# Hybrid decoder layer: the state-space stage rearranged between engines, and the low halves of the weights on VectorE

## The chip, the core and the metric

The kernel runs on one core of one Trainium2 chip. That core has TensorE (PE in the profile, with PEld for its weight loads), VectorE (DVE), ScalarE (ACT), GpSimd (POOL), SyncE (SP, which here only issues DMAs) and DMA queues. Each engine works through its own instructions in order and waits on semaphores for the others. The metric is the time of one execution in device microseconds. The kernel before takes 1495.65 us, the median of three runs from 1494.98 to 1497.01 us.

## The reference

The layer takes x of 512 tokens by 1024 channels, float32:

```
h = rms_norm(x); u = h @ w_in                  # 1024 x 11512
y_a = dsa(u)     # 16 heads, each query sees 128 keys picked by an index
y_b = nsa(u)     # 16 heads: compressed, selected and window branches
y_c = ssd(u)     # state space: 32 heads of 64, 4 groups, chunks of 128 tokens
x = x + (sig(g_a) * y_a@Wa + sig(g_b) * y_b@Wb + sig(g_c) * y_c@Wc) @ w_out
x = x + relu(rms_norm(x) @ w_1)^2 @ w_2
```

The part around the change is the state-space branch:

```
xbc  = silu(causal_conv(xbc, w, width 4) + b)      # per channel
a_cum = cumsum(dt * a) within a chunk
lmat = exp(where(i >= j, a_cum[i] - a_cum[j], -inf))
y    = (C B^T * lmat * dt) @ x  +  exp(a_cum) * (C @ h_in)  +  x * d_skip
y    = rms_norm(y * silu(z))
```

## The kernel before

All large products are computed in three passes: both operands are split into a high part (type fp32r, a rounded float32) and a low part, the remainder, and `mm3` (L316 to L319) issues high x high, high x low (or low x high) and the other mixed product into one PSUM tile `pj` of 128x512. Weights are streamed. SP issues the DMA of a tile of up to 128x1024 (`wraw`, 3 buffers), `split` (L139 to L153) makes `whi` on ACT (L150) and `wlo = wraw - whi` on POOL (L151), 6 buffers each, three tiles ahead of the use. There are 212 such tiles.

Two streams of instructions are merged into one program. The **filler** is all large products in a fixed list (`FORD`, then merge gates, branches, w_out, feed-forward): a chunk of it is eight tiles of 128 rows times three passes, 24 matmuls into one of two `pj` buffers. The **main stream** is the index of the first attention (DVE-heavy, L722 to L733), that attention (16 units), the state-space stage (16 units of one group and one chunk of tokens), and the second attention (32 units). Program order comes from a debt: each yield of the main stream gives a number of ns, which the filler works off. A scheduler then orders each engine's instructions by a priority (the main stream's is raised by `HM`) and by its own model of times. At run time those orders are fixed, and only semaphores move the engines against each other.

The filler's convolution `conv` (L676 to L700) works on one `pj` of 128 channels by 512 tokens. ACT copies it to `craw` (L679) and makes the first tap (L681), after which `pj` is free; DVE adds three taps from `craw` (L684, in SBUF), ACT makes a tanh (L686), DVE the product (L688), and for most channels PE transposes the result.

A state-space unit has three stages. `stage1` loads: `E`, 128x8x128, is a broadcast of the cumulated sums; `xs`, `zs`, and B and C. `stage2`: PE multiplies C and B into a `pT` tile, DVE multiplies it by `tri25` (0.25 where allowed, else 0) into `cbm` (L1100); DVE subtracts the head's own sum from each of the 8 parts of `E` and takes the minimum with 0 (L1102); ACT takes the exponential of all of `E` (L1103); POOL scales `xs` to `xt`, `xw` and `xd` (L1105, L1108, L1112); DVE multiplies `E` by `cbm` (L1110). `stage3`: products with the state (L1121, L1127) and eight products `xt` x `E` (L1137), then DVE adds `xd` (L1141), the state's part `t1` (L1143) and multiplies by `zs` (L1144).

An attention unit goes back and forth: PE scores (L755, L756), DVE mask and maximum (L757), ACT exponential (L764), DVE reciprocal and scaling (L770 to L777, every fourth head on POOL, L775), PE transposes (L791), ACT and DVE the two halves (L795, L796), PE the product with the values (L803, L804). `pipeline` overlaps the scores of a unit with the rest of the one before it. After the last unit the branch `b1` stores `yt`, reads it back as `yr` (L664) and splits it (L665, L666). Branch `b1` and all that follows it can't be computed earlier.

Of the kernel before, what the change touches and what calls it, by code (L numbers as in the profile page):

```python
# [14 lines left out]
S = 512  # L15
# [21 lines left out]
def build_kernel(ctx, tc, A, out):  # L37
# [44 lines left out]
    # ------------------------------------------------------------------ constants  # L82
# [37 lines left out]
    # ------------------------------------------------------------------ weights  # L120
    class WS:
# [19 lines left out]
        def split(s):  # L141
# [9 lines left out]
            pool.tensor_tensor(lo[:, :m], r[:, :m], f(hi[:, :m]), op=ALU.subtract)  # L151
# [76 lines left out]
    # first weights run ahead of the activations  # L228
# [4 lines left out]
    # ------------------------------------------------------------------ small constants  # L233
# [31 lines left out]
    # ------------------------------------------------------------------ x -> h^T  # L265
# [19 lines left out]
    tri25 = tri("tri25", 128, 0.0, 0.25, 0, -1, 1)  # L285
# [29 lines left out]
    # ------------------------------------------------------------------ matmul helpers  # L315
# [50 lines left out]
    # ------------------------------------------------------------------ persistent attention operands  # L366
# [86 lines left out]
    # ------------------------------------------------------------------ filler: all large products  # L453
# [30 lines left out]
    def cmp_prep(u1, e1):  # L484
        """k_cmp and v_cmp operands from the raw kc, vc columns."""
# [189 lines left out]
    # ------------------------------------------------------------------ conv + silu of the SSD inputs  # L675
    def conv(m, p):  # L676
        cw = lambda k: convc[:, k * 24 + m:k * 24 + m + 1]
        raw = stg.tile([128, S], F32, name="craw", tag="r", bufs=RB)
        act.activation(raw, p, AF.Copy)  # L679
        acc = stg.tile([128, S], F32, name="cacc", tag="acc", bufs=AB)  # L680
        act.activation(acc, p, AF.Identity, scale=cw(3), bias=convc[:, 96 + m:97 + m])  # L681
        for k in range(3):
            sh = 3 - k
            dve.scalar_tensor_tensor(acc[:, sh:], raw[:, :S - sh], cw(k), acc[:, sh:], op0=ALU.mult, op1=ALU.add)  # L684
        th = stg.tile([128, S], F32, name="cth", tag="th", bufs=TB)
        act.activation(th, acc, AF.Tanh, scale=0.5)  # L686
        so = raw
# [17 lines left out]
    # ------------------------------------------------------------------ DSA index and its top 128  # L705
# [33 lines left out]
    # ------------------------------------------------------------------ attention units  # L739
# [126 lines left out]
    # ------------------------------------------------------------------ NSA  # L866
# [4 lines left out]
    def cmp_a(b, g, q2, ratio):  # L871
        """Compressed-branch softmax of 8 heads and the block choice."""
# [142 lines left out]
    # ------------------------------------------------------------------ SSD  # L1015
    def ssd_prelude():
# [27 lines left out]
        for k in ("dth", "acm", "dw", "ea", "dec"):  # L1044
            sv[k] = cp.tile(n, F32, name="sv_" + k)
# [9 lines left out]
        dve.tensor_copy(sv["acm"], p[:, 0:128])  # L1055
        act.activation(sv["dec"], p[:, 128:256], AF.Exp)
# [14 lines left out]
    def ssd(sv, ratio):  # L1071
# [22 lines left out]
        def stage2(u):  # L1094
# [5 lines left out]
            dve.tensor_tensor(cbm, p[:, :128], tri25, op=ALU.mult)  # L1100
            for h in range(8):
                dve.tensor_scalar(u.E[:, h], u.E[:, h], col(sv["acm"], c, g)[:, h:h + 1], 0.0, op0=ALU.subtract, op1=ALU.min)  # L1102
            act.activation(u.E, u.E, AF.Exp)  # L1103
# [11 lines left out]
        def stage3(u):  # L1115
# [3 lines left out]
            if c:  # L1119
                po = ps("sc", [128, 512])  # L1120
                pe.matmul(po, u.b[:, 2], hst[g], start=True, stop=True)  # L1121
                t1 = sp.tile([128, 512], F32, name="t1", bufs=2)
                dve.tensor_tensor(x3(t1), x3(po), bc(col(sv["ea"], c, g)[:, :, None], [128, 8, 64]), op=ALU.mult)
                yield ratio * 858
# [16 lines left out]
            dve.tensor_tensor(yv, py, u.xd, op=ALU.add)  # L1141
            if c:
                dve.tensor_tensor(yv, yv, t1, op=ALU.add)  # L1143
# [55 lines left out]
    # ------------------------------------------------------------------ branches, merge, w_out, feed-forward  # L1199
    def branches(ya):  # L1200
# [94 lines left out]
        # w_out + residual + norm2  # L1295
# [169 lines left out]
```

## Time and profile before

| | |
|---|---|
| timed runs | 1494.98, 1495.65, 1497.01 us |
| the profiled execution: span from its first to its last instruction | 1496.3 us |
| its own time | nothing stands beside the span; it lies between the second and the third timed run |
| busy PE, PEld | 1400.1 us (94%), 1149.9 us (77%) |
| busy DVE, ACT, POOL | 1013.8 us (68%), 691.0 us (46%), 715.6 us (48%) |
| mean granted clock of TensorE | 0.978 |
| HBM traffic | 194.6 MB, 130 GB/s |

Busy is the union of an engine's instructions. PE's matmuls are pipelined and their ends are modelled, so a busy PE is not at its peak: in the feed-forward part, where nothing interrupts it, it starts a 512-wide matmul every 0.226 us (442 in 100 us). [...] A wait is idle time of an engine before an instruction, put down to what came last.

### The profile page before, as it was taken

Reading aid. Unit: us, or ns where it says so; the run is one execution under the profiler, and the core shown is the slowest. Engines: PE = TensorE matmul, PEld = TensorE weight load, DVE = VectorE, ACT = ScalarE, POOL = GpSimd, SP = SyncE. Lnnn points to the kernel's source line nnn. Section 1 sums busy time; section 2 is a strip of 40 time slices with the busy share of each in tenths; the row PEclk is TensorE's granted clock in tenths of the full one; section 3 lists DMA queues with packets and bytes.
Section 4 is the critical chain, followed back from the end, with each engine's and each line's share of the span. In section 5 each row is a group of like instructions: output and inputs, shape, how many; then the busy total and the mean of one; then the engine's idle time right before and its main releaser. Section 6 shows DMA issues by size and latency. Waiting matters only on the chain.

```text
span 1496.3 us, 19760 instructions
## 1 busy us (share of the span) xinstructions
PE 1400.1 (94%) x6832; PEld 1149.9 (77%) x6832; DVE 1013.8 (68%) x1887; ACT 691.0 (46%) x1364; POOL 715.6 (48%) x456
## 2 busy tenths in 40 slices
PE   6998999899988898899999999999999999999999
PEld 5886788677866676787788877777678888888887
DVE  4699956789789987757767898786645751433411
ACT  4545445667644454545555555545333441422220
POOL 5544534434245366544334765644753542544351
PEclk9999999999999998999999999999999999999999
DMA  5323464443565565654324744422652322323231
GB/s 194 99 77 106 150 203 130 125 122 94 139 198 173 166 199 159 200 170 130 106 89 147 206 140 117 117 78 78 211 201 82 113 99 71 127 73 112 83 106 50
DMA packets 218272, 195.92 MB, mean 131 GB/s; under 512 B 15664, under 2 KB 165564, under 8 KB 218172
## 3 DMA queue, kind: packets, MB, share of 16 engines
q1 hardware_dynamic: 212700, 183.12, 41.3%
q0 software_dynamic: 4608, 8.39, 2.0%
q10 hardware_dynamic: 864, 3.15, 0.5%
q8 instruction: 54, 0.88, 0.2%
q14 instruction: 46, 0.38, 0.1%
HBM read 157.85 MB, written 36.77 MB: 130 GB/s over the span
## 4 chain that ended last, share of the span: by engine, by line
PE 56%; DVE 29%; ACT 5%; DMA 5%; issue 4%; POOL 2%; SPq 0%; DVEq 0%; ACTq 0%; POOLq 0%
PE pj L318 15%; PE pj L319 15%; PE pj L317 15%; DVE E L1102 3%; DVE cacc L684 3%; DVE p L777 3%; ACT p L764 3%; DVE ptl L796 2%; DVE mask L731 2%; DVE m L730 1%; DVE p L757 1%; PE pT L791 1%; PE sc L1137 1%; PE sc L755 1%; DMA wraw<-in_w_in_dram 1%
## 5 line engine op out<-in xcount | busy, mean ns | idle before, releaser
L151 POOL TENSOR_TENSOR wlo<-wraw,whi 128x1024 fp32r<-128x1024 f32 (+3 forms) x212 | 479.0, 2269 | 416.7 <-ACT whi L150 394.9
L150 ACT ACTIVATE whi<-wraw 128x1024 fp32r<-128x1024 f32 (+3 forms) x212 | 207.3, 982 | 210.9 <-PE pj L319 102.1
L319 PE MATMUL pj<-hTh,wlo 128*128 128x512 f32 x384 | 156.8, 408 | 0.0
L317 PE MATMUL pj<-hTh,whi 128*128 128x512 f32 x384 | 155.4, 405 | 0.1
L318 PE MATMUL pj<-hTl,whi 128*128 128x512 f32 x384 | 154.8, 403 | 0.0
L764 ACT ACTIVATE p<-p,nb,rs 128x256 f32<-128x256 f32 (+3 forms) x192 | 123.3, 644 | 59.2 <-DVE nb L762 58.9
L317 PE MATMUL pj<-whi,hTh 128*128 128x512 f32 (+2 forms) x352 | 138.7, 396 | 8.1 <-DVE zo L575 2.2
L318 PE MATMUL pj<-wlo,hTh 128*128 128x512 f32 (+2 forms) x352 | 138.7, 395 | 0.8 <-POOL wlo L151 0.8
L319 PE MATMUL pj<-whi,hTl 128*128 128x512 f32 (+2 forms) x352 | 139.0, 396 | 0.0
L1363 DVE TENSOR_TENSOR fr<-fr 128x512 f32<-128x512 f32 x32 | 80.8, 2530 | 56.2 <-ACT fr L1362 56.2
L1371 DVE TENSOR_TENSOR x<-x,pj 128x512 f32<-128x512 f32 x32 | 22.0, 687 | 138.3 <-PE pj L319 137.8
L777 DVE TENSOR_SCALAR p<-p,rc 128x256 f32<-128x256 f32 (+3 forms) x144 | 113.3, 837 | 1.1
L775 POOL TENSOR_TENSOR p<-p,rc 128x256 f32<-128x256 f32 (+3 forms) x48 | 37.9, 790 | 152.5 <-DVE rc L770 51.8
L317 PE MATMUL pj<-yh,whi 128*128 128x512 f32 x256 | 103.4, 406 | 5.1 <-DVE gld L1282 3.1
L318 PE MATMUL pj<-yl,whi 128*128 128x512 f32 x256 | 103.6, 405 | 0.2 <-DVE yl L666 0.2
L319 PE MATMUL pj<-yh,wlo 128*128 128x512 f32 x256 | 103.0, 402 | 0.0
L318 PE MATMUL pj<-wlo,fh 128*128 128x512 f32 x256 | 99.6, 389 | 0.0
L319 PE MATMUL pj<-whi,fo 128*128 128x512 f32 x256 | 99.6, 389 | 0.0
L317 PE MATMUL pj<-whi,fh 128*128 128x512 f32 x256 | 98.8, 389 | 0.0
L319 PE MATMUL pj<-h2h,wlo 128*128 128x512 f32 (+1 forms) x256 | 96.2, 376 | 0.0
L318 PE MATMUL pj<-h2l,whi 128*128 128x512 f32 (+1 forms) x256 | 96.2, 376 | 0.0
L317 PE MATMUL pj<-h2h,whi 128*128 128x512 f32 (+1 forms) x256 | 96.1, 376 | 0.0
(333 smaller groups left out, 3322.5 us busy)
## 6 DMA issues: line engine op xcount, KB each, us to landing
wraw<-in_w_in_dram SPq DMA_DIRECT2D x84, 512.0 KB, 4.1
wraw<-in_w_ff_dram SPq DMA_DIRECT2D x64, 512.0 KB, 4.0
gld<-g_d SPq DMA_DIRECT2D x48, 256.0 KB, 3.1
q_d<-qev SPq DMA_DIRECT2D x32, 256.0 KB, 2.3
qu<-q_d POOLq DMA_DIRECT2D x32, 256.0 KB, 4.2
E<-ac_d SPq DMA_DIRECT2D x16, 512.0 KB, 4.3
wraw<-in_w_br_ssd_dram SPq DMA_DIRECT2D x16, 512.0 KB, 4.2
g_d<-gth SPq DMA_DIRECT2D x24, 256.0 KB, 2.0
```

Of the source, the lines that this page charges most:

```text
L150: act.activation(hi[:, :m], r[:, :m], AF.Copy)
L151: pool.tensor_tensor(lo[:, :m], r[:, :m], f(hi[:, :m]), op=ALU.subtract)
L317: pe.matmul(o, lh, rh, start=first, stop=False)
L318: pe.matmul(o, lh, rl, start=False, stop=False)
L319: pe.matmul(o, ll, rh, start=False, stop=last)
L684: dve.scalar_tensor_tensor(acc[:, sh:], raw[:, :S - sh], cw(k), acc[:, sh:], op0=ALU.mult, op1=ALU.add)
L731: dve.match_replace(wk, m8, wk, TAKEN)
L764: act.activation(u.p[h][:, :n], u.p[h][:, :n], AF.Exp, bias=u.nb[:, h:h + 1], scale=rs8[:, u.b, u.h0 + h:u.h0 + h + 1], accum_out=u.sm[:, ...
L775: pool.tensor_tensor(u.p[h][:, :n], u.p[h][:, :n], bc(rc[:, h:h + 1], [128, n]), op=ALU.mult)
L777: dve.tensor_scalar(u.p[h][:, :n], u.p[h][:, :n], rc[:, h:h + 1], None, op0=ALU.mult)
L1102: dve.tensor_scalar(u.E[:, h], u.E[:, h], col(sv["acm"], c, g)[:, h:h + 1], 0.0, op0=ALU.subtract, op1=ALU.min)
L1363: dve.tensor_tensor(r, r, r, op=ALU.mult)
```

## The change

Five edits. In `conv` the copy L679 goes, and the three taps read `pj` in PSUM. In the state-space unit `cbm` is made on ACT with a plain factor of 0.25; the triangle is applied to `E` by a select on POOL (fill -1e30); the head's own sum comes in as the bias of eight exponentials of 128x128 on ACT, from a new table `nac` of negated sums, in place of eight DVE instructions and one wide exponential. The skip term is added to `t1` on POOL, so that DVE adds once to the product. And `wlo` of every weight tile is computed on DVE. Line numbers after L285 are lower by one to three in the changed file.

```diff
-            pool.tensor_tensor(lo[:, :m], r[:, :m], f(hi[:, :m]), op=ALU.subtract)
+            dve.tensor_tensor(lo[:, :m], r[:, :m], f(hi[:, :m]), op=ALU.subtract)
...
-    tri25 = tri("tri25", 128, 0.0, 0.25, 0, -1, 1)
...
-        raw = stg.tile([128, S], F32, name="craw", tag="r", bufs=RB)
-        act.activation(raw, p, AF.Copy)
         acc = stg.tile([128, S], F32, name="cacc", tag="acc", bufs=AB)
...
-            dve.scalar_tensor_tensor(acc[:, sh:], raw[:, :S - sh], cw(k), acc[:, sh:], op0=ALU.mult, op1=ALU.add)
+            dve.scalar_tensor_tensor(acc[:, sh:], p[:, :S - sh], cw(k), acc[:, sh:], op0=ALU.mult, op1=ALU.add)
...
-        so = raw
+        so = stg.tile([128, S], F32, name="craw", tag="r", bufs=RB)
...
+        dve.tensor_scalar(sv["nac"], p[:, 0:128], -1.0, None, op0=ALU.mult)
...
-            dve.tensor_tensor(cbm, p[:, :128], tri25, op=ALU.mult)
+            act.activation(cbm, p[:, :128], AF.Copy, scale=0.25)
+            pool.affine_select(out=u.E, in_=u.E, compare_op=ALU.is_ge, fill=NEG, base=0,
+                               pattern=[[0, 8], [1, 128]], channel_multiplier=-1)
             for h in range(8):
-                dve.tensor_scalar(u.E[:, h], u.E[:, h], col(sv["acm"], c, g)[:, h:h + 1], 0.0, op0=ALU.subtract, op1=ALU.min)
-            act.activation(u.E, u.E, AF.Exp)
+                act.activation(u.E[:, h], u.E[:, h], AF.Exp, bias=col(sv["nac"], c, g)[:, h:h + 1])
...
                 dve.tensor_tensor(x3(t1), x3(po), bc(col(sv["ea"], c, g)[:, :, None], [128, 8, 64]), op=ALU.mult)
+                pool.tensor_tensor(t1, t1, u.xd, op=ALU.add)
...
-            dve.tensor_tensor(yv, py, u.xd, op=ALU.add)
-            if c:
-                dve.tensor_tensor(yv, yv, t1, op=ALU.add)
+            dve.tensor_tensor(yv, py, t1 if c else u.xd, op=ALU.add)
             dve.tensor_tensor(yv, yv, u.zs, op=ALU.mult)
```

The scheduler orders all engines anew. Numbers in the names below tell buffers apart. On DVE, in the state-space stage, one unit's work stood like this before:

```order
L1141 TENSOR_TENSOR yv_4432<-sc_4390,xs_4184 128x512
L1143 TENSOR_TENSOR yv_4432<-yv_4432,t1_4393 128x512
L1144 TENSOR_TENSOR yv_4432<-yv_4432,zs_4186 128x512
L1100 TENSOR_TENSOR cbm_4362<-pT_4360,tri25_269 128x128
L1110 TENSOR_TENSOR E_4275<-E_4275,cbm_4362 128x1024
L1102 TENSOR_SCALAR E_4350<-E_4350,sv_acm_663 128x128 x8
```

and in the changed program, where `t1` already holds the skip term:

```order
L1122 TENSOR_TENSOR t1_5305<-sc_5303,sv_ea_662 128x512
L1109 TENSOR_TENSOR E_5110<-E_5110,cbm_5199 128x1024
L473 TENSOR_TENSOR qev_5867<-pF_5856,qev_5867 64x2x128
L151 TENSOR_TENSOR wlo_6358<-wraw_6170,whi_6357 128x1024
L1141 TENSOR_TENSOR yv_5333<-sc_5302,t1_5305 128x512
L1142 TENSOR_TENSOR yv_5333<-yv_5333,zs_5114 128x512
```

The eight instructions on `E`, `cbm` and the second addition have left DVE, and a `wlo` stands in it. The second place is DVE in the first attention, where the convolutions run between attention work. Before, the three taps of a chunk (L684) read `craw`:

```order
L684 SCALAR_TENSOR_TENSOR cacc_3946<-craw_3944,convc_297,cacc_3946 128x509
L688 SCALAR_TENSOR_TENSOR craw_3895<-cth_3902,cacc_3897 128x512
L684 SCALAR_TENSOR_TENSOR cacc_3946<-craw_3944,convc_297,cacc_3946 128x510
L796 TENSOR_TENSOR ptl_3246<-pT_3240,pth_3245 128x512
L811 TENSOR_TENSOR yt_3201<-pv_3161,yt_3201 64x512
L684 SCALAR_TENSOR_TENSOR cacc_3946<-craw_3944,convc_297,cacc_3946 128x511
```

Now (as L681) they read `pj`:

```order
L681 SCALAR_TENSOR_TENSOR cacc_3933<-pj_3894,convc_294,cacc_3933 128x509
L754 ISA p_3019,mx_3015<-sc_3018,mask1_696 128x256
L754 ISA mx_3015 128x1
L759 SCALAR_TENSOR_TENSOR nb_2929<-mx_2928,rs8_322 128x4
L681 SCALAR_TENSOR_TENSOR cacc_3933<-pj_3894,convc_294,cacc_3933 128x510
L767 RECIPROCAL rc_2920<-smx_2810 128x4
L685 SCALAR_TENSOR_TENSOR craw_3892<-cth_3890,cacc_3885 128x512
L681 SCALAR_TENSOR_TENSOR cacc_3933<-pj_3894,convc_294,cacc_3933 128x511
```

The `pj` buffer is now released by the last of the three, with attention work of other units between them, where ACT alone released it before. The third place is PE at the end of the second attention. Before, the scores of the last unit (`qu_9996`) and the products with the values stand among the filler's matmuls into `pj`, which go on behind them:

```order
L755 MATMUL sc_10467<-kh_s1_307,qu_9996 128x128
L756 MATMUL sc_10467<-kl_s1_308,qu_9996 128x128
L803 MATMUL pv_10397<-pth_10447,v_s1_314 128x512
L804 MATMUL pv_10397<-ptl_10448,v_s1_314 128x512
L318 MATMUL pj_9765<-yl_9759,whi_9593 128x512
L319 MATMUL pj_9765<-yh_9758,wlo_9594 128x512
L318 MATMUL pj_9792<-yl_9759,whi_9662 128x512
L319 MATMUL pj_9792<-yh_9758,wlo_9663 128x512
```

In the changed program the last unit ends like this, and the next `pj` is the first of branch `b1`:

```order
L788 MATMUL pT_10531<-ident_105,p_10475 128x128 x2
L940 MATMUL pv_10508<-cph_10267,vz_321 128x128 x4
L800 MATMUL pv_10508<-pth_10518,v_w1_313 128x512
L801 MATMUL pv_10508<-ptl_10519,v_w1_313 128x512
L800 MATMUL pv_10508<-pth_10536,v_s1_311 128x512
L801 MATMUL pv_10508<-ptl_10537,v_s1_311 128x512
L316 MATMUL pj_10567<-yh_10483,whi_10015 128x512
L316 MATMUL pj_10568<-yh_10483,whi_10067 128x512
```

Between the last `pj` of branch `b0` and that first one of `b1`, PE has 120 attention matmuls in a row; before, no more than 22 stand together anywhere. Counted in matmuls into `pj` that stand ahead, the first attention starts at 751 (before: 662), the state-space products at 1416 (1306), the second attention at 1928 (1776), and its last product with the values stands at 2880 (2856), where `b0` ends at 2880 in both.

## Rows read from the trace of the kernel before

**Rows 1.** Windows: length, busy us of PE, PEld, DVE, ACT, POOL, clock, DMA, GB/s.

```profile
60.00:200.00 140.00, 126.91 (x651) 104.68 (x650) 129.10 (x291) 63.84 (x140) 67.58 (x38) 0.98 0.40 121
...
200.00:420.00 220.00, 208.73 (x1040) 171.79 (x1038) 164.51 (x340) 138.04 (x279) 89.56 (x58) 0.99 0.50 134
...
420.00:640.00 220.00, 188.41 (x911) 148.53 (x912) 190.17 (x300) 107.16 (x218) 121.19 (x79) 0.91 0.62 181
...
860.00:1060.00 200.00, 186.46 (x912) 150.91 (x911) 167.20 (x351) 101.30 (x228) 115.76 (x85) 0.97 0.39 112
...
1004.00:1072.00 68.00, 63.09 (x307) 50.38 (x306) 45.90 (x111) 32.68 (x83) 38.54 (x34) 0.97 0.44 127
...
1200.00:1300.00 100.00, 100.00 (x442) 82.80 (x442) 39.22 (x29) 30.30 (x39) 45.02 (x19) 1.00 0.30 95
```

**Rows 2.** Waits of PE, 420 to 640 us: total us, times, longest.

```profile
PE pT L1127 <- DVE cbm L1100: 14.1, 3, 7.1
...
PE pT L1150 <- DVE hst L1133: 6.8, 3, 4.1
...
PE sc L1137 <- DVE E L1110: 3.7, 2, 3.4
```

**Rows 3.** Timeline of DVE in the state-space stage: start, us, line, operation.

```profile
474.19 0.69 DVE L1143 TENSOR_TENSOR yv<-yv,t 128x512 f32<-128x512 f32 x1
...
476.20 1.22 DVE L1110 TENSOR_TENSOR E<-E,cbm 128x1024 f32<-128x1024 f32 x1
...
482.70 0.74 DVE L684 SCALAR_TENSOR_TENSOR cacc<-craw,convc,cacc 128x509 f32<-128x509 f32 x1
...
493.46 2.43 DVE L1102 TENSOR_SCALAR E<-E,sv_acm 128x128 f32<-128x128 f32 x8
...
556.92 9.30 DVE L1102 TENSOR_SCALAR E<-E,sv_acm 128x128 f32<-128x128 f32 x8
```

**Rows 4.** Timeline of POOL beside the last of rows 3.

```profile
559.30 2.35 POOL L151 TENSOR_TENSOR wlo<-wraw,whi 128x1024 fp32r<-128x1024 f32 x1
...
562.61 2.33 POOL L151 TENSOR_TENSOR wlo<-wraw,whi 128x1024 fp32r<-128x1024 f32 x1
```

**Rows 5.** DVE groups by form: count, busy us, mean ns, idle before.

```profile
L1363 DVE TENSOR_TENSOR fr<-fr 128x512 f32<-128x512 f32 x32 | 80.8, 2530 | 56.2 <-ACT fr L1362 56.2
...
L796 DVE TENSOR_TENSOR ptl<-pT,pth 128x512 fp32r<-128x512 f32 x95 | 64.2, 681 | 3.6 <-ACT pth L795 3.4
...
L1102 DVE TENSOR_SCALAR E<-E,sv_acm 128x128 f32<-128x128 f32 x128 | 61.7, 552 | 7.4 <-DMA E<-ac_d 7.3
...
L684 DVE SCALAR_TENSOR_TENSOR cacc<-craw,convc,cacc 128x510 f32<-128x510 f32 x24 | 24.4, 1018 | 0.3
...
L1282 DVE SCALAR_TENSOR_TENSOR gld<-gld,pj 128x512 f32<-128x512 f32 x24 | 16.3, 681 | 12.7 <-DMA gld<-g_d 7.5 <-POOL mixf L1285 3.3 <-PE pj L319 1.9
...
L1143 DVE TENSOR_TENSOR yv<-yv,t 128x512 f32<-128x512 f32 x12 | 15.2, 1270 | 0.3
...
L757 DVE CUSTOM_DVE_ANT_0 p<-sc,caus 128x128 f32<-128x128 f32 x48 | 13.2, 281 | 7.8 <-PE sc L756 7.7
```

**Rows 6.** POOL groups by form.

```profile
L151 POOL TENSOR_TENSOR wlo<-wraw,whi 128x1024 fp32r<-128x1024 f32 x172 | 420.8, 2456 | 382.4 <-ACT whi L150 360.7 <-DVE rc L772 14.0 <-DMA wraw<-in_w_in_dram 4.1
...
L261 POOL TENSOR_SCALAR_AFFINE_SELECT caus<-caus 128x512 f32<-128x512 f32 x1 | 0.6, 612 | 0.0
```

**Rows 7.** ACT groups by form.

```profile
L764 ACT ACTIVATE p<-p,nb,rs 128x128 f32<-128x128 f32 x48 | 23.1, 482 | 12.3 <-DVE nb L762 12.2
...
L1153 ACT ACTIVATE yev<-pT,gcol 128x128 f32<-128x128 f32 x64 | 18.2, 367 | 2.8 <-PE pT L1150 2.8
```

**Rows 8.** Timelines of PE, SP and DVE where attention ends.

```profile
1060.06 0.39 PE L804 MATMUL pv<-ptl,v_s 128*128 128x512 f32 x1
...
1066.19 0.81 SPq L664 DMA_DIRECT2D yr<-yb_d  x2
...
1070.08 1.48 DVE L666 TENSOR_TENSOR yl<-yr,yh 128x512 fp32r<-128x512 f32 x2 [1.44 <-ACT yh L665]
```

More of the change, by code (lines that the diff above doesn't have):

```diff
@@ L1043, in ssd_prelude @@
         sv = {}
-        for k in ("dth", "acm", "dw", "ea", "dec"):
+        for k in ("dth", "acm", "dw", "ea", "dec", "nac"):
             sv[k] = cp.tile(n, F32, name="sv_" + k)
```

## The prediction

> **What bounds the kernel now.** I read the busy totals first: PE works 1400.1 us of a span of 1496.3, so what can be won is its 96 us of idle time and the stretches in which its clock is down, and nothing that an engine does beside a busy PE costs anything. Then the windows [rows 1], to see where PE lacks. In the feed-forward part (1200 to 1300 us) PE is busy all of the 100 us while DVE is busy for 39. In the state-space stage (420 to 640 us) PE idles 220 - 188.4 = 31.6 us, the clock is 0.91, and DVE is the busiest engine with 190.2. The first attention (200 to 420) idles 11.3 us, the second one's later half (860 to 1060) 13.5, the index stage (60 to 200) 13.1 with DVE busy for 129 of 140. Third, PE's waits in the state-space stage: 14.1 us on `cbm`, 6.8 on `hst` and 3.7 on `E`, 24.6 together and all DVE's [rows 2]. Fourth, DVE's timeline there, to see why DVE is late: eight L1102 take 2.43 us at one place, and 9.30 at another [rows 3], where POOL runs two `wlo` of 2.3 us each in the same time [rows 4]. By groups, L1143 means 1.27 us against 0.69 free, L684 1.02 against 0.74, L1102 0.55 against 2.43/8 = 0.30 [rows 3, 5]. So DVE is not only loaded there, it is held up while POOL works in SBUF. Last, the timelines where attention ends, for what must run before branch `b1` can start [rows 8].
>
> **State-space stage.** DVE loses L1102, 61.7 us, and the second addition, 15.2 us [rows 5]; the sixteen small multiplications into `cbm` come to little. It gains `wlo`. The filler brings one tile per 24 matmuls, and in the changed program 1928 - 1416 = 512 matmuls into `pj` stand in this stage, so 21 tiles. The same operation and size on DVE free is L1110, 1.22 us [rows 3]: 26 us. DVE then has 190 - 62 - 15 + 26 = 139 of 220 us, with the holds by `wlo` gone besides. What the work costs elsewhere: ACT does 128 exponentials of 128x128; L1153 with its per-partition operand has 0.367 us, L764 with a bias and a sum 0.482 [rows 7], so 47 to 62 us in place of 16 wide ones, on an engine with 107 of 220 busy. POOL does 16 selects; the nearest row is one of 128x512 at 0.61 us [rows 6], so an estimated 1.0 to 1.3 us for 128x1024, and twelve additions at about half a `wlo` (1.2 us), 30 to 36 us, and it loses about 20 `wlo` of 2.46. Both stay far from full.
>
> The path to `sc` L1137 now goes through ACT and POOL rather than DVE, but it starts at `stage2`, one stage ahead of its use, and has eight exponentials of 0.4 us and a select in it, 4 to 5 us, where before it had 2.4 to 9.3 us of L1102 and a wide exponential. I take 22 of the 24.6 us of waits on DVE back, and 10 us of the clock: 188 us of busy PE at 0.91 rather than at 0.97, the level of the windows around, are 11 us. Together -32. The bounds are -14 (half of the waits, no more than 2 of the clock: POOL's new work holds DVE up as `wlo` did) and -40 (all of the waits, and 15 of the clock).
>
> [...]
>
> **The rest of the split.** In the feed-forward part `wlo` moves from POOL to DVE. L1363 takes 2.53 us each time [rows 5], beside a `wlo`; without it I expect about 0.7. Either way DVE has 39 of 100 us there and PE none idle: 0. If that cover were gone it would show as waits of L316 on `wlo`. In the index stage DVE is nearly full: 20 or so tiles of 1.22 us are 24 us more, against holds that vanish (there PE runs ahead of nothing but filler, and its idle time is 13.1 us). I take 0, bounds -6 (half of that idle time) and +10 (DVE's surplus of 24 less the 11 us that it has free). In the second attention, 1080 filler matmuls (1776 to 2856 before) are 45 tiles, 55 us of DVE, against holds of about that size if they are to its work as in the rows of L684 and L1143 (0.3 to 0.6 us on an instruction of 0.7). I take -6, about half of 13.5; bounds -12 and +6.
>
> **The convolution.** Reading PSUM, a tap should cost what L1282 costs, 0.68 us, against 0.74 from SBUF when free [rows 3, 5], so 72 taps are 4 us cheaper on DVE; ACT loses 24 copies. [...] What matters is the release of `pj`. It was ACT's copy and tap; now DVE's third tap is the last reader, and in the order an attention's mask, reciprocal and bias stand between the taps. There are only two `pj`, and PE fills the other in about 24 x 0.23 = 5.4 us, so a release that is late by less than that costs nothing. Three taps with what lies between are 3 to 4 us when DVE is on time. I charge 0.3 us on each of 24 chunks, +7; bounds 0 and 1.5 us on each, +36 (DVE late by two instructions of 0.7).
>
> **The end of attention.** The main stream stands later against the filler everywhere (751 against 662 matmuls at the first attention, 1928 against 1776 at the second), and at the end the filler runs out: 120 attention matmuls in a row, behind them the store of `yt`, the load `yr`, its split, and only then `b1`'s second half. Before, from the last product L804 (1060.06 us) to the end of the split (1071.56) were 11.5 us [rows 8], under which `b0`'s last matmuls lay. Now the tail holds some 5.5 units. A unit's steps per head block are a mask of 0.28 us, an exponential of 0.48, ACT's and DVE's halves of the transposes (0.68), scaling and small ones between [rows 5, 7]; overlapped by `pipeline` I take 5.5 us per unit, the larger engine's sum, so 30 us, with 14 us of PE work in them: 16 lost. The chain of 11.5 us is covered by the twelve first-half matmuls (2.7 us): 8 or 9 lost. Of what 1004 to 1072 us loses now, 4.9 us idle and some clock [rows 1], 7 us go. Net +17. Bounds +8 (units run beside each other) and +37 (they run singly, below).
>
> **Sum.** Against the profiled span of 1496.3 us: -32 - 6 + 0 + 7 + 17 = -14, so 1482.3. The timed median lies 0.65 below that span, inside the spread of the runs; 1482 is what I predict.
>
> **Rivals.**
> - *More won than forecast.* If the holds were the whole reason why DVE is late, everything behind them falls: -40 in the state-space stage, -12 in the second attention, +10 at the end, 0 for the convolution: -42, 1454. For it speaks that nearly all PE waits end on DVE; against it, the 120 matmuls that nothing can cover. Chance 0.15.
> - *Slower: the end of attention runs uncovered.* The units of the tail run one after the other: per unit four masks (1.1), four exponentials (1.9), scalings (1.2), the transposes' halves (1.4) and waits between engines (2.2), 7.8 us, six of them 47 us, with 14 of PE work: 33 lost. With 12 for the chain and its start, less 8 that go, +37 in place of +17, and with an unchanged rest 1502. It decides if the tail costs more than 31 us, where the sum reaches zero. For it: no filler at all is left there, and attention works back and forth between engines. Against: `pipeline` keeps two units going. Chance 0.17.
> - *Slower: the convolution holds `pj`.* With 1.5 us on each of 24 chunks, +36 in place of +7: 1511. It decides from 0.9 us a chunk. For it: DVE has 164 of 220 us busy in the first attention, PE only 11 idle, so it can only lose. Against: the other buffer covers 5.4 us. Chance 0.10.
> - *The change doesn't relieve DVE.* The selects and additions on POOL hold it up as `wlo` did, and half of the gain stays away: -14 instead of -32, 1500. For it: an operation of POOL of the same type and size held L1102 up. Against: 36 us of POOL work in place of 50, and less on DVE that can be held. Chance 0.10.
>
> **How the numbers follow.** The forecast has 0.48, with a range of its own of 1468 to 1492. From run to run this kernel differs by about 0.2%, 3 us, and less than that can't be told from no change. Faster: 0.44 of the forecast and all 0.15 of the first rival, 0.59. Same: 0.04 of the forecast, 0.04 each of the tail and of the fourth rival, 0.12. Slower: 0.13, 0.10 and 0.06, 0.29. The range goes to 1456 below, near the first rival, and to 1510 above, which takes in the tail and the fourth and leaves out most of the third.
>
> **What would show it.** In the profile after: PE's idle time in the state-space stage (from the place where `pT` L1127's counterpart starts to appear) near 8 us, its clock over 0.95, and no wait over 2 us on `cbm` or `E`; `wlo` on DVE at 1.2 us; the product `fr` at 0.7. For the convolution: waits of PE's L316 on DVE's L681, 7 us in sum and not 36. At the end: about 30 us in which PE does attention only, idle about half, then 8 us before `yl` is there. Wrong would be: PE's waits in the state-space stage now on ACT or POOL (`E`) with 20 us or more; `wlo` late for PE in the index stage, where DVE is full; or an idle time of over 31 us around the last attention unit.

## The result, and the profile after

The changed kernel takes 1448.51 us (median of four runs, 1441.28 to 1449.42) against 1495.32: a ratio of 0.968, with a 95% interval from 0.965 to 0.970. It is 47 us faster. I had forecast 1482 and a range that ended at 1456, so the direction held and the size did not. The profiled execution has a span of 1446.1 us, 50 below that of before.

The windows of the kernel after, with the columns of [rows 1]:

```profile
60.00:200.00 140.00, 134.88 (x699) 112.67 (x697) 130.66 (x304) 67.01 (x141) 20.22 (x14) 0.99 0.41 126
200.00:420.00 220.00, 216.95 (x1088) 180.46 (x1089) 182.17 (x395) 139.26 (x278) 22.41 (x32) 0.99 0.51 138
420.00:640.00 220.00, 210.49 (x1070) 170.19 (x1069) 138.34 (x174) 135.41 (x350) 129.13 (x97) 0.98 0.75 222
860.00:1060.00 200.00, 183.03 (x864) 147.48 (x865) 155.44 (x364) 102.42 (x229) 58.42 (x49) 0.92 0.40 122
980.00:1020.00 40.00, 31.69 (x129) 25.14 (x128) 25.83 (x100) 22.80 (x66) 6.25 (x8) 0.66 0.23 68
1200.00:1300.00 100.00, 100.00 (x443) 82.84 (x442) 41.47 (x46) 29.16 (x36) 0.00 (x0) 1.00 0.36 105
```

In the state-space stage PE idles 9.5 us where it idled 31.6, at a granted clock of 0.98 of full speed in place of 0.91, and DVE is busy for 138 of 220 (I had 139). But the first window, the index stage, has won too, and so has the first attention: PE idles 5 and 3 us there where it idled 13 and 11. The stretch that is new is 980 to 1020 us, the end of attention, with 8 us idle and a clock of 0.66.

PE's waits in the state-space stage, 420 to 640 us:

```profile
PE pT L1096 <- DMA bcx<-BC_d: 3.1, 3, 1.1
PE sc L1137 <- DVE E L1109: 2.2, 1, 2.2
...
PE pT L1148 <- DVE hst L1133: 1.1, 1, 1.1
```

The waits on `cbm` are gone, those on `hst` and `E` are 3.3 us in place of 10.5 [rows 2]. DVE by forms:

```profile
L151 DVE TENSOR_TENSOR wlo<-wraw,whi 128x1024 fp32r<-128x1024 f32 x172 | 221.1, 1289 | 129.4 <-ACT whi L150 120.3 <-DMA rs_d<-rt 4.8 <-PE pv L801 1.3
...
L774 DVE TENSOR_SCALAR p<-p,rc 128x512 f32<-128x512 f32 x36 | 26.7, 790 | 0.3
...
L1361 DVE TENSOR_TENSOR fr<-fr 128x512 f32<-128x512 f32 x32 | 21.9, 685 | 0.0
...
L681 DVE SCALAR_TENSOR_TENSOR cacc<-pj,convc,cacc 128x511 f32<-128x511 f32 x24 | 17.9, 744 | 0.5
L681 DVE SCALAR_TENSOR_TENSOR cacc<-pj,convc,cacc 128x510 f32<-128x510 f32 x24 | 17.7, 738 | 0.1
...
L722 DVE SCALAR_TENSOR_TENSOR mask<-irelu,iwt,mask 128x512 f32<-128x512 f32 x7 | 5.2, 737 | 0.0
```

`wlo` means 1.29 us, and `fr` 0.685, where L1363 had 2.53 [rows 5]. Two of these forms of the kernel before I had not put among my rows, the scaling in the attention and the accumulation in the index:

```profile
L777 DVE TENSOR_SCALAR p<-p,rc 128x512 f32<-128x512 f32 x36 | 40.9, 1188 | 0.3
...
L725 DVE SCALAR_TENSOR_TENSOR mask<-irelu,iwt,mask 128x512 f32<-128x512 f32 x7 | 7.1, 1007 | 0.0
```

Both have become a quarter to a third shorter (0.79 and 0.74 us). In the experiments below the scaling takes 1.14 to 1.38 us wherever `wlo` stays on POOL (e2, e3, e3r, e5) and 0.73 to 0.79 wherever it is moved (e1, wc, e4), so it was held. For the mask the order counts too: it takes 0.75 us in e2 and 0.76 in e5, with `wlo` still on POOL.

To see which stage won what, I take the **loss** of a stretch: its length less the sum, over PE's matmuls in it, of the median time from the start of such a matmul to the next start (0.227 us for the large ones), with the medians of the kernel after. A loss holds idle time and slow clock together. The index stage is counted from 40 us. The stages are cut at the first score of the first attention, 8 us before the first state-space product, at the last one, and 75 us before and 35 us after the last product with the values. Worked out so from the traces, in us, one profiled execution each (e1 to h32_bh4 are the experiments below, by the head of their names). The profiled executions of e1 and e3r lie 5 and 4 us below their timed medians and that of r1 5 us above, so a few us in a column are no difference:

| kernel | timed median | ratio to before, 95% | index | first attention | state space | second attention | end | all else |
|---|---|---|---|---|---|---|---|---|
| before | 1495.3 | 1 | 21.6 | 18.7 | 48.2 | 21.8 | 12.3 | 15.8 |
| after | 1448.5 | 0.965 to 0.970 | 12.6 | 6.0 | 13.2 | 13.0 | 26.4 | 16.8 |
| e1 | 1457.9 | 0.970 to 0.975 | 11.4 | 0.9 | 25.1 | 13.5 | 26.4 | 15.5 |
| e2 | 1490.9 | 0.995 to 0.999 | 19.8 | 17.1 | 42.5 | 21.7 | 12.6 | 19.6 |
| e3 | 1493.2 | 0.996 to 1.000 | 21.6 | 15.5 | 29.4 | 35.0 | 14.6 | 19.1 |
| e3r | 1482.8 | 0.987 to 0.993 | 21.3 | 15.6 | 28.0 | 23.0 | 14.0 | 17.2 |
| e5 | 1463.4 | 0.975 to 0.980 | 19.5 | 9.9 | 19.4 | 23.9 | 13.2 | 17.1 |
| wc | 1463.2 | 0.971 to 0.979 | 11.6 | 7.7 | 25.0 | 21.2 | 25.7 | 14.3 |
| e4 | 1457.8 | 0.972 to 0.976 | 12.0 | 1.1 | 18.3 | 25.1 | 25.7 | 15.6 |
| e4r | 1453.5 | 0.968 to 0.975 | 11.3 | 1.0 | 18.2 | 20.7 | 24.3 | 15.1 |
| j2 | 1570.1 | 1.046 to 1.051 | 48.6 | 17.9 | 34.9 | 50.4 | 31.8 | 27.4 |
| j3 | 1508.0 | 1.005 to 1.009 | 24.2 | 8.0 | 30.4 | 32.0 | 29.6 | 22.2 |
| r1 | 1447.8 | 0.966 to 0.970 | 12.0 | 4.5 | 17.6 | 17.4 | 24.7 | 16.0 |
| h32 | 1450.1 | 0.966 to 0.971 | 21.3 | 2.3 | 19.2 | 6.3 | 25.3 | 15.3 |
| bh4 | 1453.8 | 0.968 to 0.974 | 12.3 | 7.8 | 16.2 | 14.3 | 32.9 | 13.8 |
| h32_bh4 | 1463.7 | 0.974 to 0.980 | 21.4 | 3.1 | 14.0 | 21.1 | 30.3 | 14.4 |

From before to after: index -9, first attention -13, state space -35, second attention -9, end +14, all else +1; together -50, the difference of the spans.

PE's waits of over 0.15 us, added up over the whole trace by the engine that ended them, go the same way: those on VectorE are 80.5 us before and 37.7 after; in e2, e3 and e5, which leave `wlo` on POOL, 78.2, 73.1 and 50.6; in e1, wc and e4, which move it, 41.9, 46.6 and 33.1.

### The profile page after: what moved, and what is told of

Its sections match the earlier page's. It is cut to its first block, busy times and chain, and to the rows that moved or that the text cites. A ratio compares the mean times of both kernels' runs of the same rounds, so it can differ in the third digit from the quotient of the medians.

```text
span 1446.1 us, 19744 instructions
## 1 busy us (share of the span) xinstructions
PE 1392.2 (96%) x6832; PEld 1150.7 (80%) x6832; DVE 973.5 (67%) x1944; ACT 707.0 (49%) x1468; POOL 300.1 (21%) x270
## 4 chain that ended last, share of the span: by engine, by line
PE 67%; DVE 13%; DMA 9%; issue 4%; ACT 3%; POOL 3%; SPq 1%; DVEq 0%; POOLq 0%; ACTq 0%
PE pj L316 18%; PE pj L317 18%; PE pj L318 18%; DMA gld<-g_d 3%; DVE wlo L151 2%; PE pT L788 2%; PE sc L753 2%; PE sc L752 1%; DVE p L774 1%; PE pv L801 1%; PE pv L800 1%; DVE p L754 1%; DMA wraw<-in_w_in_dram 1%; DMA E<-ac_d 1%; ACT p L761 1%
## 5 line engine op out<-in xcount | busy, mean ns | idle before, releaser
L151 DVE TENSOR_TENSOR wlo<-wraw,whi 128x1024 fp32r<-128x1024 f32 (+3 forms) x212 | 257.1, 1216 | 133.3 <-ACT whi L150 124.1
L317 PE MATMUL pj<-h2l,whi 128*128 128x512 f32 (+1 forms) x256 | 96.3, 376 | 0.0
L316 PEld LDWEIGHTS pj<-hTh,whi 128*128 128x128 f32 x384 | 73.0, 190 | 17.7 <-issue 2.4
L318 PEld LDWEIGHTS pj<-hTh,wlo 128*128 128x128 f32 x384 | 72.7, 189 | 16.5 <-issue 2.2
```

Source lines behind the costliest of these rows:

```text
L151: dve.tensor_tensor(lo[:, :m], r[:, :m], f(hi[:, :m]), op=ALU.subtract)
L316: pe.matmul(o, lh, rh, start=first, stop=False)
L317: pe.matmul(o, lh, rl, start=False, stop=False)
L318: pe.matmul(o, ll, rh, start=False, stop=last)
```

## The experiments

**One edit at a time.** Theory H: GpSimd's `wlo` held VectorE up in every stage, and taking it off GpSimd is most of the gain. Theory S, my forecast: the state-space edits carry it.

*e1: the kernel before, `wlo` on VectorE.*

```diff
-            pool.tensor_tensor(lo[:, :m], r[:, :m], f(hi[:, :m]), op=ALU.subtract)
+            dve.tensor_tensor(lo[:, :m], r[:, :m], f(hi[:, :m]), op=ALU.subtract)
```

> The kernel before with one edit: wlo of every weight tile on VectorE. Nothing else changes. By stages, the changed kernel won 9 us in the index stage, 13 in the first attention, 35 in the state-space stage, 9 in the second attention, and lost 14 at the end of attention. Theory H (the wlo on GpSimd held VectorE up in every stage, and moving it off is most of the gain): index -9, first attention -9 or more although the convolution is unchanged, state-space -15 to -20 although its instructions are unchanged, second attention -8, end of attention +10 (98 attention matmuls stand in a row there); together -30 to -36, 1459 to 1465 us. Theory S (my forecast: the gain is the work that the state-space edits take off VectorE; elsewhere wlo on VectorE costs what the holds cost): index 0, first attention 0, state-space -8, second attention 0 to -6, end +10; together -4 to +2, 1491 to 1497 us.

Measured: 1457.9 us, -38 (0.973). One line of the five edits gives four fifths of the gain, and the first attention, with the old convolution, loses 0.9 us in place of 18.7. Its windows, columns as above:

```profile
200.00:420.00 220.00, 219.02 (x1109) 182.56 (x1108) 184.47 (x393) 150.99 (x301) 21.57 (x32) 1.00 0.52 141
420.00:640.00 220.00, 203.41 (x1025) 162.40 (x1024) 179.05 (x334) 106.44 (x218) 90.26 (x68) 0.98 0.70 212
```

With every L1102 still on DVE, its state-space stage is at a clock of 0.98 and PE idles 16.6 us, half of before. H holds, S falls. One rival to H is that `wlo` was merely ready sooner on VectorE. The trace of the kernel before speaks against it, since PE hardly waited for `wlo` there, 0.8 us in all:

```profile
L318 PE MATMUL pj<-wlo,hTh 128*128 128x512 f32 (+2 forms) x352 | 138.7, 395 | 0.8 <-POOL wlo L151 0.8
```

*e2: the kernel before, taps from PSUM, no copy.*

```diff
-        act.activation(raw, p, AF.Copy)
...
-            dve.scalar_tensor_tensor(acc[:, sh:], raw[:, :S - sh], cw(k), acc[:, sh:], op0=ALU.mult, op1=ALU.add)
+            dve.scalar_tensor_tensor(acc[:, sh:], p[:, :S - sh], cw(k), acc[:, sh:], op0=ALU.mult, op1=ALU.add)
```

> The kernel before with one edit: the convolution's taps read pj in PSUM, ScalarE's copy is gone. wlo stays on GpSimd. Theory C (a tap with one source in PSUM is not held up by GpSimd, so the edit itself won a good part of the first attention's 13 us): first attention -6 to -10, the mean of a tap near 0.7 us in place of 1.02, 1485 to 1489 us. Forecast's step (pj is released later, by VectorE's third tap): first attention +7, waits of TensorE's first pass on the tap, 1502 us. Theory H has nothing for this edit alone: within 3 us of 1495.

Measured: 1490.9, -5, outside all three expectations (it lies between theory C's and theory H's). The taps of e2, though `wlo` is still on POOL:

```profile
L682 DVE SCALAR_TENSOR_TENSOR cacc<-pj,convc,cacc 128x511 f32<-128x511 f32 x24 | 17.9, 744 | 0.4
L682 DVE SCALAR_TENSOR_TENSOR cacc<-pj,convc,cacc 128x510 f32<-128x510 f32 x24 | 17.8, 741 | 0.4
```

0.74 us against a mean of 1.02 before for the middle one [rows 5]: these taps, with their source in PSUM, are not held. The mechanism of theory C is so shown, but its place is not: the first attention won only 1.6 us.

*e3: the state-space edits alone; e3r: the same with the debts of the second attention at 2.0 in place of 2.5, which changes nothing but the order there.*

```diff
-            dve.tensor_tensor(cbm, p[:, :128], tri25, op=ALU.mult)
+            act.activation(cbm, p[:, :128], AF.Copy, scale=0.25)
...
+                act.activation(u.E[:, h], u.E[:, h], AF.Exp, bias=col(sv["nac"], c, g)[:, h:h + 1])
```

> The kernel before with the state-space edits alone (mask by select on GpSimd, factor on ScalarE, sum as bias of the exponential, skip term on GpSimd). wlo stays on GpSimd, the convolution keeps its copy. Theory S: the work taken off VectorE (62 + 15 us) is the gain: state-space stage -25 to -32, everything else 0, 1464 to 1470 us. Theory H: VectorE stays held by wlo, and by the selects and additions that GpSimd now does besides; state-space -12 to -18, GpSimd itself close to full there (121 us before, +36): 1478 to 1484 us.

> The state-space edits alone, as in the run of that name, with the main stream's yields of the second attention counted 2.0 times in place of 2.5; the work is the same, only the order of the second attention differs. There the state-space edits had won 19 us in their own stage and the second attention lost 13 more than before. Theory O (that loss is an accident of the order): the second attention loses 20 to 25 us to the ideal rate, 1478 to 1484 us. Theory H (with wlo on GpSimd VectorE is held in the second attention whatever the order): 30 us or more, 1489 to 1496 us.

Measured: 1493.2 and 1482.8. Both win 19 to 20 us in their own stage, a little more than theory H had and less than theory S, and POOL is busy for 161 of the 189 us of that stage in e3. The total of e3 is above both of its expectations, that of e3r is what theory O expected. e3 gives the gain back in the second attention, which the edits don't touch; with another order of the same instructions there it is 12 us better. In e3, PE waits there for VectorE's scaling (610 to 980 us):

```profile
PE pT L790 <- DVE p L776: 9.1, 6, 2.2
PE sc L754 <- DVE mx L756: 5.3, 6, 2.0
```

In e3r the first of these is 4.6 us. So some 10 us hang on the order alone, and single edits can't be told apart to less than that.

**What each edit adds to the others.**

*e5: the changed kernel with `wlo` back on GpSimd. wc: `wlo` and convolution without the state-space edits. e4: the changed kernel with the old convolution; e4r: that with debts of 2.0.* Each is one of the three pieces above, put in or taken out.

> The changed kernel with wlo back on GpSimd (state-space edits and convolution from PSUM stay). The attention's end has no stretch of attention matmuls alone in this order (as before the change). Theory H: what is missing against the changed kernel (1448.5) is the index stage 9, second attention 9, part of the first attention and 15 in the state-space stage, less the 14 of the end of attention that come back: 1468 to 1475 us. Theory S: nearly all of the gain stays and the end costs nothing: 1440 to 1450 us.

> The kernel before with wlo on VectorE and the convolution from PSUM; the state-space stage as before. Theory S' (the state-space edits still give something on top: 13 us of loss in their stage against 25 with wlo alone): 1457 to 1462 us. Theory H' (with wlo off GpSimd the old state-space stage is nearly as good, and what the edits win there is lost in the order elsewhere): 1447 to 1453 us.

> The changed kernel with the convolution as before (ScalarE's copy, taps from SBUF). With wlo alone moved, the first attention lost only 1 us to the ideal rate of TensorE, in the changed kernel 6. Theory K (my step was right: pj released by VectorE's third tap costs 5 to 7 us): the first attention loses 1 us again, nothing else moves, 1442 to 1445 us. Theory C (with a source in PSUM a tap is cheaper and can't be held): taps at 0.74 us again, the first attention loses 8 to 10, 1451 to 1454 us.

> The changed kernel with the old convolution, and the second attention's yields counted 2.0 times. Without that it was 9 us slower than the changed kernel, of which the first attention won 5 and the second attention, where no convolution runs, lost 12. Theory O (the second attention's part is an accident of the order): 13 to 18 us lost there in place of 25, and 60 attention matmuls alone at the end in place of 120; 1444 to 1450 us, so the convolution's edit is worth nothing by itself here. Theory C (the edit frees VectorE and ScalarE of something that is felt later): 1455 to 1460 us.

Measured: 1463.4, 1463.2, 1457.8 and 1453.5. All four were missed by both theories: e5 and e4r came out between them, wc above both, e4 has K's first attention (1.1 us of loss) and with it a total worse than C's. What moving `wlo` brings, by pairs: 38 us on the kernel before, 28 on the convolution (e2 to wc), 29 to 35 on the state-space edits (e3r to e4r, e3 to e4), 15 on both (e5 to after). The state-space edits bring 2 to 13 alone, 28 on top of the convolution, 0 to 4 on top of `wlo`, 15 on top of both. The convolution brings 5 alone, loses 5 on top of `wlo` alone, brings 19 to 30 on top of the state-space edits (e3r to e5, e3 to e5), and 5 to 9 on top of the rest. Only the first is clear in every pair. With `wlo` left on GpSimd, the other edits together still bring 32 of the 47 us (e5). The gains don't add up, as one expects where edits relieve the same engine, and the order's 10 us lie over the small ones.

**The holds themselves.** *j2: the changed kernel, and GpSimd repeats the subtraction. j3: the changed kernel, and GpSimd adds `whi` and `wlo` in pieces into a tile that nobody reads.* Both add work without a use.

```diff
             dve.tensor_tensor(lo[:, :m], r[:, :m], f(hi[:, :m]), op=ALU.subtract)
+            pool.tensor_tensor(r[:, :m], r[:, :m], f(hi[:, :m]), op=ALU.subtract)              # j2
...
+                pool.tensor_tensor(junk[:, :e - j], f(lo[:, j:e]), f(hi[:, j:e]), op=ALU.add)  # j3
```

> The changed kernel, and GpSimd repeats every subtraction of wlo behind VectorE's, in place in wraw, 2.4 us each; nobody reads it. So GpSimd works in SBUF as before the change, while VectorE's wlo and all else stay. Theory H (holds): VectorE's instructions with two sources in SBUF are long again (wlo itself, the mask's and the state-space's additions, fr at 2.5 us), and index, attention and state-space stage lose what they had won, 25 to 40 us; in this order 54 attention matmuls stand alone at the end in place of 120, which gives 5 to 8 back: 1465 to 1485 us. Theory W (the gain of moving wlo came from its being made sooner, not from VectorE's running free): 1440 to 1450 us. The weight buffers come free about 4 us later, which by the three buffers and 5.4 us per tile should not show.

> The changed kernel, and after each wlo GpSimd adds whi and wlo in eight pieces of 128 columns into a tile of its own that nobody reads. It touches no wraw, so no weight is loaded later, and the order of TensorE is nearly that of the changed kernel (122 attention matmuls alone at the end). Theory H (holds are the cause): VectorE's instructions on two SBUF sources or in SBUF alone are long again beside it, taps from PSUM stay at 0.74 us; index, attention and state-space stage lose 30 us or more together: over 1480 us. Theory W (the 121 us of the second subtraction came from weights that were loaded later): within 10 us of 1448.

Measured: 1570.1 and 1508.0, 122 and 60 us slower than the changed kernel. j3 gives back all that the change had won, on DVE's own program unchanged and an order of PE nearly the same. Rows of j3 on DVE and, last, on POOL:

```profile
L1365 DVE TENSOR_TENSOR fr<-fr 128x512 f32<-128x512 f32 x32 | 30.4, 951 | 0.0
...
L685 DVE SCALAR_TENSOR_TENSOR cacc<-pj,convc,cacc 128x511 f32<-128x511 f32 x24 | 17.8, 743 | 0.5
...
L726 DVE SCALAR_TENSOR_TENSOR mask<-irelu,iwt,mask 128x512 f32<-128x512 f32 x7 | 5.9, 839 | 0.0
```

```profile
L155 POOL TENSOR_TENSOR junk<-wlo,whi 128x128 f32<-128x128 f32 x1548 | 910.0, 588 | 208.1 <-DVE wlo L151 92.4 <-DVE cm L917 5.8 <-DVE nb L763 1.9
```

`fr` and the mask are longer again (0.95 and 0.84 against 0.69 and 0.74), the taps from PSUM are not (0.74), and the first attention, where the taps run, loses only 2 us more. So work of GpSimd that nobody reads costs 60 us, and it makes VectorE's instructions longer. That the 60 us come by way of VectorE is not shown by j3: PE's waits on VectorE rise by only 9 us against the changed kernel (46.9 against 37.7), those on ACT by 13, on DMAs by 11 and on POOL by 7. These pieces take POOL 910 us, twice what `wlo` took, so its own work comes later (POOL is busy for 200 of 220 us in the state-space stage, and stands in front of the select), and they hold the buffers of `whi`: ACT waits 59.8 us for them before its next `whi`. In the first attention 8.0 us of loss is far from the 17.1 of e2, whose taps read PSUM too; the pieces are short, and how much each holds up was not taken apart. In j2 the subtraction comes on top of VectorE's own `wlo`, which then takes 1.62 us. There PE's waits on VectorE do rise, to 96.3 us, which is 59 of the 80 us by which PE idles longer than in the changed kernel. The total, 1570.1, lies far above theory H's 1465 to 1485; the rest of it, clock and other waits, was not taken apart.

**The end of attention.** *r1: debts of 1.3, 1.8 and 0.3 for the three stages. h32: `wlo` of the first 32 tiles on GpSimd. bh4: four tiles of `b1` begun early (`BH = 4`). h32_bh4: both, with debts of 1.2, 1.6 and 0.3.*

```diff
-R0, R1, R2, R3 = 1000.0, 1.5, 2.5, 0.5
+R0, R1, R2, R3 = 1000.0, 1.3, 1.8, 0.3   # r1
...
-            dve.tensor_tensor(lo[:, :m], r[:, :m], f(hi[:, :m]), op=ALU.subtract)
+            (pool if i < 32 else dve).tensor_tensor(lo[:, :m], r[:, :m], f(hi[:, :m]), op=ALU.subtract)   # h32
```

> The changed kernel with three constants of the merge: the main stream's yields of the first attention count 1.3 times (before 1.5), of the second 1.8 (2.5), of the state-space stage 0.3 (0.5), so that less filler runs ahead of the main stream. The order then has 39 attention matmuls alone at the end in place of 120. Theory T (the end of attention loses 14 us because the filler has run out, and only the order's place decides it): the end loses 10 to 14 us less, the stages before 0 to 4 more: 1436 to 1442 us. Theory M (the main stream is late for reasons of its own, VectorE's work, and packing it tighter opens waits inside the stages): 1446 to 1452 us.

> The changed kernel with wlo of the first 32 tiles on GpSimd (they last to about the end of the index stage), the other 180 on VectorE. In this order the first attention starts at filler matmul 662 as before the change, and no attention matmuls stand alone at the end. Theory T (VectorE's 24 us more in the index stage push the main stream back, and the end of attention pays): index stage loses 20 us again (+8), end of attention 12 to 13 in place of 26 (-14): 1440 to 1445 us. Theory M: the end stays at 20 us or more, 1452 to 1458 us.

> The changed kernel with four instead of two tiles of branch b1 begun on the half of the operand that is there early: 24 matmuls, not 12, under the store, load and split of the last half, which is 2.7 us more of cover. Theory T (the end loses what the chain after the last product lasts beyond its cover): 2 to 4 us less at the end, 1444 to 1447 us. Theory M (the wait moves behind the tiles that are begun): 1448 us.

> All that the runs so far point to in one kernel: the change, wlo of the first 32 tiles on GpSimd (the main stream starts 13 us earlier), four tiles of b1 begun early, and debts of 1.2, 1.6 and 0.3 (19 attention matmuls alone at the end). Theory T: index stage 8 more than in the changed kernel, end of attention 10 to 14 less, the rest as there: 1436 to 1443 us. Theory M (the filler runs out where the main stream ends, whatever the order, as in the two runs that tried each alone): 1445 to 1451 us.

Measured: 1447.8, 1450.1, 1453.8 and 1463.7. None is clearly faster than the changed kernel, and h32_bh4 is 15 us slower. Theory T fell each time; theory M's time was met by r1 alone (h32 lies between the two, bh4 and h32_bh4 above both). r1 has 39 attention matmuls alone at the end in place of 120, h32 has none, and both lose 25 us there. In h32 the wait has moved behind the last product (1000 to 1030 us):

```profile
PE pj L316 <- ACT yh L664: 9.2, 2, 7.3
PE pT L788 <- DVE p L774: 2.7, 1, 2.7
```

So the stretch without cover is the same whether it stands ahead of the last product or behind it: the filler is used up when the main stream ends. In bh4 the 12 matmuls more are paid with a wait of 7.7 us for `gld`, in the same stretch of bh4, whose cause was not taken apart:

```profile
PE pj L316 <- DVE gld L1280: 7.7, 1, 7.7
PE pj L316 <- ACT yh L664: 4.2, 1, 4.2
```

## Why the prediction was wrong, step by step

**The step that failed is "the rest of the split"**, with the term that was missing for the first attention. I took 0 for the index stage, because 24 us of `wlo` on a full DVE would outweigh the holds that go; measured -9. `wlo` in the windows 60 to 200 and 420 to 640 us of the kernel after:

```profile
60.00:200.00 140.00, 26.95 (x23) 0.99 0.41 126
420.00:640.00 220.00, 37.02 (x24) 0.98 0.75 222
```

27 us of `wlo` went into the first window, and DVE's busy time there rose by 130.66 - 129.10 = 1.6 us [rows 1]. But the stage ends at 201 us before and at 214 after, so the windows don't hold the same work. From 60 us to its end DVE is busy for 129.1 us before and 140.4 after, of which 28.3 are `wlo`: 17 us of holds went, and 11 us were added. So VectorE did get more work than it was relieved of, as I had it, and the stage became 13 us longer. What failed was to set VectorE's balance against PE's idle time and get 0. PE had filler to run in the longer stage (673 matmuls into `pj` from 40 us to its end, in place of 576), and what had cost it time were waits on VectorE for the filler's own results (L474, L575, L411): its waits on VectorE in this stage are 12.2 us before and 3.5 after.

In the first attention I charged the convolution 7 and gave nothing for the holds, although L684 at 1.02 against 0.74 stood in my own rows; e1 shows what that term was worth, 18.7 - 0.9 = 18 us. The run h32 separates the stages: it has `wlo` of the index stage on GpSimd and starts the first attention at filler matmul 662, as before the change. Its index stage loses 21.3 us, as before, and its first attention 2.3. These two steps make -9 and -13 where I had 0 and +7: 29 of the 36 us by which the span was missed. My first rival named the mechanism and had 1454, with a chance of 0.15; but its sum had nothing for these two stages either, and came near by taking more in the others.

**State-space stage, -32:** -35, with the waits and the clock about as worked out. The way there was only half mine. I worked it out from the work taken off DVE, with the holds of `wlo` "gone besides"; alone that work is worth 19 us of the stage (e3), `wlo` alone 23 (e1), and together 30 (e4) to 35. And in the changed kernel VectorE is still held there: the `wlo` of the window above take 1.54 us each where I had 1.22 (1.23 in the window 1200 to 1300 us, where POOL does nothing), with POOL busy for 129 of 220 us where it was for 121. That DVE's 138 us match my 139 is luck in part, since `wlo` takes 37 of them and not 26. The eight exponentials took 0.387 us each (median), between my 0.367 and 0.482.

**Second attention, -6:** -9, in a kernel where the order moves this stage by 12.

**The convolution, +7:** the direction was right where `wlo` is on VectorE, and the size at the upper end. The first attention loses 0.9 to 1.1 us with the copy (e1, e4, e4r) and 2.3 to 7.8 without (h32 2.3, h32_bh4 3.1, r1 4.5, after 6.0, wc 7.7, bh4 7.8). Whether `pj`'s late release is its cause the waits don't show: PE's wait on `cacc` there is 0.7 us. The tap itself takes 0.74 us, as from SBUF when free, and not the 0.68 that I read from L1282. What the step lacked is that a tap from PSUM keeps its 0.74 us beside `wlo` on POOL (e2), which is worth something only as long as POOL works there (e5's first attention 9.9 against e3's 15.5, e2's 17.1 against 18.7 before).

The taps from PSUM stay at 0.74 us both beside `wlo` on POOL (e2) and beside POOL's pieces (j3). And POOL can be the longer one too. Its addition into `mixf` took 1.34 us before and takes 1.56 after:

```profile
L1285 POOL TENSOR_TENSOR mixf<-mixf,gld 128x512 f32<-128x512 f32 x32 | 43.0, 1344 | 29.9 <-DVE gld L1284 18.1 <-DVE gld L1282 4.1 <-PE pT L791 3.2
```

```profile
L1283 POOL TENSOR_TENSOR mixf<-mixf,gld 128x512 f32<-128x512 f32 x32 | 49.9, 1563 | 86.3 <-DVE gld L1282 41.3 <-DVE gld L1280 18.9 <-DVE rc L769 14.2
...
L1099 POOL TENSOR_SCALAR_AFFINE_SELECT E<-E 128x1024 f32<-128x1024 f32 x16 | 20.2, 1266 | 58.5 <-DMA xs<-xs_d 30.9 <-DMA E<-ac_d 27.5 <-ACT qev L472 0.2
```

In the trace of the kernel after, the longer of the two is the one that starts second. Four of these additions that start 0.15 to 0.17 us behind a `wlo` of 1024 columns on DVE (778.22, 781.14, 791.32 and 824.84 us) take 2.18 to 2.20 us, and that `wlo` takes 1.21 or 1.22. Three that start 0.11 to 0.44 us ahead of such a `wlo` (787.33, 814.06 and 850.01 us) take 1.28 or 1.29, and that `wlo` takes 1.94 to 2.26.

The select (the last row above) took 1.27 us, inside the 1.0 to 1.3 that I had estimated.

**The end of attention, +17:** +14, but put together otherwise. I counted the 11.5 us of [rows 8] as a chain; when everything waits for it, it is 4.9 us from the last product (L801) to the end of the split, read from PE, ACT and DVE:

```profile
1013.11 0.63 PE L801 MATMUL pv<-ptl,v_s 128*128 128x512 f32 x1
1016.58 0.79 PE L316 MATMUL pj<-yh,whi 128*128 128x512 f32 x1 [2.84 <-ACT yh L664]
```

```profile
1015.90 1.39 ACT L664 ACTIVATE yh<-yr 128x512 fp32r<-128x512 f32 x2 [1.53 <-DMA yr<-yb_d]
```

```profile
1016.56 1.45 DVE L665 TENSOR_TENSOR yl<-yr,yh 128x512 fp32r<-128x512 f32 x2 [1.48 <-ACT yh L664]
```

PE waits only 2.8 us for it. From 980 to 1020 us the loss is 21 us. PE idles for 8 of them, and the other 13 are the clock, 0.66 in that window (matmuls of 128x512 start every 0.43 us at 1018.02 to 1018.88 us, and every 0.23 at 1019.91 to 1020.60), which I had left out of this term. And the cause that I gave, the order's 120 matmuls, is not what decides (r1, h32).

**The rivals.** The tail that runs uncovered and the convolution that holds `pj` did not come true in their size. The fourth, that POOL's new work holds DVE up as `wlo` did, is there in kind: L1142 means 0.96 us in the changed kernel and takes 0.67 to 0.69 where POOL does nothing beside it (444.27, 535.45, 606.36 and 613.79 us), but PE's waits are not on it.

## What to carry to other kernels

When one instruction turns out to be held up by another engine, sum that up over every form that shows a mean above its free time, in every stage, before any edit is priced: here one line that moved the cause brought 38 us, more than the other edits together (32). And set what an engine gains or loses against the waits of the engine that bounds the kernel: an index stage that became longer cost PE no time there, because PE had other work to run in it. In a kernel whose order comes from a scheduler, the same work in another order differs by 10 us of 1490, so that a part of a change is measured in several orders or not at all below that.

## What had not been expected of the hardware

In e1, where nothing else changed, VectorE took over 247 us of `wlo` and its busy time rose by 2, from 1013.8 to 1016.1 us: by my estimate from these numbers, some 245 us of its busy time had been holds. Its busy share before, 68%, said little of its load. And a GpSimd instruction of 128 columns cost 0.59 us beside VectorE's work (j3), so that 1024 columns in eight pieces took 4.7 us, where one `wlo` of 1024 had taken 2.46 before the change.
